# One adaLN unit less ahead of the first main step, the fold matrix first on VectorE, and matmuls on ones in three places

## The chip, the cores and the metric

The kernel runs on one core of a Trainium2 chip. Five engines of the core work side by side, each through its own queue in program order: TensorE (PE in the profile, with its weight loads listed apart as PEld), VectorE (DVE), ScalarE (ACT), GpSimd (POOL) and SyncE (SP), which issues the transfers from the chip's main memory. An engine waits only where its next instruction waits for a semaphore. The metric is the device time of one execution in microseconds (us), lower is better. Three runs of the kernel before took 1697.41, 1698.73 and 1699.22 us, so the median is 1698.73 us.

## The reference

Two layers of a diffusion backbone over 256 latent tokens and 256 context tokens of width 1024, all in float32. Layer 0 mixes tokens with a Conformer convolution, layer 1 with a bidirectional mLSTM; each is followed by a squared-ReLU MLP. What matters here is how a layer begins: a vector of shifts, scales and gates (adaLN) is computed from a conditioning vector by one large matrix, and the tokens are modulated with it before the first product.

```python
def adaln(cvec, w, b):
    return jnp.split(jax.nn.silu(cvec) @ w + b, 6, axis=-1)

def modulate(x, shift, scale):
    return x * (1 + scale) + shift

def conformer_conv(u, rows, w_pw1, b_pw1, w_dw, b_dw, ln_g, ln_b, w_pw2, b_pw2):
    a = u @ w_pw1 + b_pw1
    a = a[..., :CONV_DIM] * jax.nn.sigmoid(a[..., CONV_DIM:])
    ...
    a = jax.nn.silu(layer_norm(a + b_dw, ln_g, ln_b))
    return a @ w_pw2 + b_pw2

for i in range(DEPTH):
    ...
    sh1, sc1, g1, sh2, sc2, g2 = adaln(c[:, None, :], ada_w[i], ada_b[i])
    u = modulate(h, sh1, sc1)
```

## The kernel before

Activations lie transposed in SBUF: eight tiles of 128 channels by 512 tokens (latent and context side by side). A product in float32 accuracy is made of three matmuls on operands split into a high and a low part (`mm3`): high weight by high data, high weight by low data, low weight by high data. `split` makes such a pair: ScalarE copies the source to the high part (`wh` for weights), VectorE subtracts to get the low part (`wl`).

**The opening** works through eight units f, one for each 128 input channels. For a unit, SyncE issues three transfers: `raw`, the 128x2048 piece of the adaLN matrix for this unit's shift and scale; `x`, its 128x512 tokens; and `F`, a 128x512 piece of the first weight matrix `pw1`. Then

- `start0` runs eight float32 matmuls of 32 columns (`ada_mm`, the rows `fl<-raw,cs`), and VectorE copies the sum to SBUF (`F<-fl`);
- `start1` folds the four row groups of that sum with two small matmuls against the matrix `fold` (`ada_fold`, the rows `ln<-fold,F`); VectorE adds the biases (`sh1p`, `sc1p`); ScalarE makes the high part of the modulated tokens (`u`, two halves) while VectorE makes a full copy (`S`) and from it the low part (`u<-S,u`); the weight piece is split too;
- `start2` is the main step: four output tiles m (`ps0`, three PSUM tiles tagged `mm` and one tagged `cv`), three matmuls of 128x512 each, twelve in all.

The loop in the kernel before issues fold f-1, unit f's adaLN matmuls, and main step f-2, in this order, and `pin` fixes PE's order to that of the code. So three units' adaLN matmuls and two folds stand ahead of the first main step. The other engines' orders come from a scheduler; VectorE's also takes in the work of lower priority that follows (`foldg`, `pc`, and the sine tables `tab`). The tile pools set when transfers may start: `raw` has three buffers and `F` five.

After the opening the remaining twelve output tiles of `pw1` follow, 24 matmuls each, with transposes and small products between them.

**The place of the later waits** is the end of the convolution. VectorE ends a token normalisation (`mv`), it and ScalarE apply it (`apply_norm`), PE turns the result by transposes (`silu`, the rows `ln<-ident,u`), ScalarE applies SiLU and splits, and the products with `pw2` start in the PSUM tile `lead2[0]`. Just ahead of the transposes PE runs the last adaLN matmuls of this layer (`ada_s2.mm`, eight of them on tiles `S` and `L`).

## Time and profile before

| | us |
|---|---|
| median of three runs | 1698.73 |
| the profiled execution, whole | 1699.18 |
| its span, first to last instruction | 1697.5 |
| PE busy in the span | 1669.2 |
| DVE busy | 1033.0 |
| ACT busy | 744.0 |

The 1.7 us between the span and the whole time of the profiled execution lie before its first and after its last instruction. A row of the timeline gives the start in us from the span's start, the duration (of a row with "xN", that of N instructions merged), the engine, the line, the operation, what is written and read, and in brackets how long the engine had been idle and what ended it. A float32 matmul is shown as two instructions, so `x16` for the eight adaLN matmuls of a unit. The durations of matmuls overlap, since they are pipelined; what one costs in a row of equals is the distance of their starts. A row of the windows view gives, for a stretch of time, its length, each engine's busy time with the number of instructions, the granted PE clock (1.00 is full), the busy share of the transfer engines, and the GB/s they moved.

### The profile page before, as it was taken

Reading aid. Unit: us, or ns where it says so; the run is one execution under the profiler, and the core shown is the slowest. Engines: PE = TensorE matmul, PEld = TensorE weight load, DVE = VectorE, ACT = ScalarE, POOL = GpSimd, SP = SyncE. Lnnn points to the kernel's source line nnn. Section 1 sums busy time; section 2 is a strip of 40 time slices with the busy share of each in tenths; the row PEclk is TensorE's granted clock in tenths of the full one; section 3 lists DMA queues with packets and bytes.
Section 4 is the critical chain, followed back from the end, with each engine's and each line's share of the span. In section 5 each row is a group of like instructions: output and inputs, shape, how many; then the busy total and the mean of one; then the engine's idle time right before and its main releaser. Section 6 shows DMA issues by size and latency. Waiting matters only on the chain.

```text
span 1697.5 us, 22796 instructions
## 1 busy us (share of the span) xinstructions
PE 1669.2 (98%) x8878; PEld 1363.8 (80%) x8878; DVE 1033.0 (61%) x1841; ACT 744.0 (44%) x1195; POOL 44.3 (3%) x92
## 2 busy tenths in 40 slices
PE   7999999999999999999999999999999999999997
PEld 5655898878888998876788899888877878878886
DVE  5555795666645776751243653563487786776676
ACT  3312563232324476642333533442477564645443
POOL 0000000000000000000000000000011120000001
PEclk9999999999999999999999999999999999999999
DMA  8546322434424065567765752454454556756552
GB/s 340 198 156 243 111 75 95 157 128 146 145 100 148 2 211 180 183 238 252 251 214 174 251 181 105 155 189 171 157 190 176 193 195 209 257 211 229 192 184 89
DMA packets 70828, 300.54 MB, mean 177 GB/s; under 512 B 7170, under 2 KB 22018, under 8 KB 40384
## 3 DMA queue, kind: packets, MB, share of 16 engines
q1 hardware_dynamic: 53056, 284.39, 47.6%
q10 hardware_dynamic: 17664, 14.69, 2.7%
q8 instruction: 70, 1.15, 0.3%
q14 instruction: 38, 0.31, 0.1%
HBM read 283.32 MB, written 15.73 MB: 176 GB/s over the span
## 4 chain that ended last, share of the span: by engine, by line
PE 92%; DVE 5%; ACT 1%; issue 1%; DMA 1%; POOL 0%; SPq 0%; DVEq 0%; POOLq 0%; ACTq 0%
PE mm L175 17%; PE mm L178 17%; PE mm L179 17%; PE mm L190 7%; PE mm L191 4%; PE mm L206 3%; PE mm L207 3%; PE mm L208 3%; PE cv L208 2%; PE cv L207 2%; PE cv L206 2%; PE fl L335 1%; DVE wl L153 1%; PE fl L748 1%; PE cv L830 1%
## 5 line engine op out<-in xcount | busy, mean ns | idle before, releaser
L153 DVE TENSOR_TENSOR wl<-raw,wh 128x1024 fp32r<-128x1024 f32 x346 | 424.7, 1233 | 275.8 <-ACT wh L152 271.4
L152 ACT CAST wh<-raw 128x1024 fp32r<-128x1024 f32 x346 | 360.6, 1050 | 494.5 <-PE mm L178 269.0
L178 PE MATMUL mm<-u,wh 128*128 128x512 f32 (+1 forms) x808 | 292.9, 363 | 0.1
L175 PE MATMUL mm<-u,wh 128*128 128x512 f32 (+1 forms) x680 | 245.5, 361 | 0.2 <-ACT E L770 0.2
L179 PE MATMUL mm<-u,wl 128*128 128x512 f32 (+1 forms) x680 | 242.3, 357 | 0.0
L178 PEld LDWEIGHTS mm<-u,wh 128*128 128x128 f32 x808 | 153.4, 190 | 23.5 <-issue 1.8
L175 PEld LDWEIGHTS mm<-u,wh 128*128 128x128 f32 x680 | 129.2, 190 | 28.8 <-issue 9.1
L179 PEld LDWEIGHTS mm<-u,wl 128*128 128x128 f32 x680 | 129.2, 190 | 18.4 <-issue 0.2
L175 PE MATMUL mm<-xm,wh 128*128 128x512 f32 x256 | 102.2, 399 | 0.0
L206 PE MATMUL mm<-wh,xl 128*128 128x512 f32 x256 | 101.3, 396 | 0.5 <-ACT wh L152 0.5
L207 PE MATMUL mm<-wh,xl 128*128 128x512 f32 x256 | 100.9, 394 | 0.0
L179 PE MATMUL mm<-xm,wl 128*128 128x512 f32 x256 | 99.9, 390 | 0.0
L208 PE MATMUL mm<-wl,xl 128*128 128x512 f32 x256 | 99.6, 392 | 0.0
L175 PE MATMUL mm<-hid,wh 128*128 128x512 f32 (+1 forms) x256 | 93.1, 364 | 0.0
L178 PE MATMUL mm<-hid,wh 128*128 128x512 f32 (+1 forms) x256 | 92.8, 363 | 0.0
L179 PE MATMUL mm<-hid,wl 128*128 128x512 f32 (+1 forms) x256 | 92.7, 362 | 0.0
L190 PE MATMUL mm<-x,wh 128*128 128x512 f32 x232 | 81.0, 398 | 0.8 <-DVE x L1698 0.8
L416 DVE SCALAR_TENSOR_TENSOR S<-ar,cs,S 128x512 f32<-128x512 f32 x56 | 40.8, 749 | 61.3 <-DMA ar<-ada_w 61.0
L178 PE MATMUL mm<-qq,wh 128*128 128x272 f32 x256 | 73.9, 289 | 0.0
L175 PE MATMUL mm<-qq,wh 128*128 128x272 f32 x256 | 73.5, 289 | 0.0
L179 PE MATMUL mm<-qq,wl 128*128 128x272 f32 x256 | 73.5, 288 | 0.0
L190 PE MATMUL mm<-u,wh 128*128 128x512 f32 x192 | 68.6, 399 | 0.0
(507 smaller groups left out, 3277.8 us busy)
## 6 DMA issues: line engine op xcount, KB each, us to landing
raw<-w SPq DMA_DIRECT2D x64, 1024.0 KB, 4.8
raw<-wo SPq DMA_DIRECT2D x32, 1024.0 KB, 4.9
raw<-ada_w SPq DMA_DIRECT2D x26, 1024.0 KB, 5.9
ar<-ada_w SPq DMA_DIRECT2D x80, 256.0 KB, 3.4
raw<-wv SPq DMA_DIRECT2D x16, 1024.0 KB, 5.4
raw<-wqT SPq DMA_DIRECT2D x16, 1024.0 KB, 5.6
raw<-wq SPq DMA_DIRECT2D x16, 1024.0 KB, 4.9
raw<-wk SPq DMA_DIRECT2D x16, 1024.0 KB, 5.2
```

What stands on the lines that cost most here:

```text
L152: c = nc.scalar.copy(hi, src)
L153: nc.vector.tensor_tensor(lo, src, hi.bitcast(F32), op=ALU.subtract)
L175: a = nc.tensor.matmul(ps, wh, xh, start=start, stop=False)
L178: nc.tensor.matmul(ps, wh, xl, start=False, stop=False)
L179: lastmm[0] = nc.tensor.matmul(ps, wl, xh, start=False, stop=stop).ins
L190: todo = [lambda s_, e_: nc.tensor.matmul(ps, wh, r[0], start=s_, stop=e_), lambda s_, e_: nc.tensor.matmul(ps[:, :n], wl, r[0][:, :n], st ...
L191: lambda s_, e_: nc.tensor.matmul(ps[:, :n], wl, r[0][:, :n], start=s_, stop=e_)]
L206: nc.tensor.matmul(ps, xh, wh, start=start, stop=False)
L207: nc.tensor.matmul(ps, xl, wh, start=False, stop=False)
L208: nc.tensor.matmul(ps, xh, wl, start=False, stop=stop)
L335: a = nc.tensor.matmul(ps[32 * j:32 * j + 32], cs[:, kt, 14 - 2 * v:46 - 2 * v], blocks[kt], start=first and kt < 4, stop=last and kt >= 4 ...
L416: nc.vector.scalar_tensor_tensor(a, w, c, a, op0=ALU.mult, op1=ALU.add)
```

## The change

Six edits, all in the order of work; no product of the reference is added or taken away.

1. The opening's loop issues adaLN 0, fold 0, adaLN 1 and then, for each f, the first three matmuls of main step f, fold f+1, the other nine, and adaLN f+2. Two units' adaLN matmuls and one fold stand ahead of the first main step.
2. `idle(ps, n)` issues n matmuls of the 128x128 tile `ones` by itself into a PSUM tile that nobody reads before it is overwritten: 13 ahead of adaLN 0, 3 ahead of fold 0, 5 ahead of adaLN 1.
3. `foldg`, which is used much later, moves to the work of low priority, and the copy of the adaLN sum may not be issued on VectorE before `fold` is complete.
4. The weight piece is split after that copy and before the biases, which now wait in the order for the split's subtraction.
5. The fold's matmuls are fixed in PE's order.
6. At the end of the convolution `lead2` is allocated earlier, and five matmuls on ones go behind the last adaLN matmul, three more behind the turn of block 3.

```diff
@@ -136,12 +136,7 @@
     fold = con.tile([P, 16], F32, name="fold")
     nc.vector.tensor_tensor(fold, ident[:, 0:16], ident[:, 32:48], op=ALU.add)
     for j in (2, 3):
-        nc.vector.tensor_tensor(fold, fold, ident[:, 32 * j:32 * j + 16], op=ALU.add)
-    foldg = con.tile([P, 16], F32, name="foldg")
-    nc.vector.tensor_tensor(foldg, ident[:, 0:16], ident[:, 16:32], op=ALU.add)
-    for j in range(2, 8):
-        nc.vector.tensor_tensor(foldg, foldg, ident[:, 16 * j:16 * j + 16], op=ALU.add)
-
+        folded = nc.vector.tensor_tensor(fold, fold, ident[:, 32 * j:32 * j + 16], op=ALU.add).ins
 
     def raw_load(src):
         raw = wp.tile([P, 2048], F32, tag="raw", name=nm("raw"), bufs=3)
@@ -150,9 +145,10 @@
 
     def split(hi, lo, src):
         c = nc.scalar.copy(hi, src)
-        nc.vector.tensor_tensor(lo, src, hi.bitcast(F32), op=ALU.subtract)
+        lastsub[0] = nc.vector.tensor_tensor(lo, src, hi.bitcast(F32), op=ALU.subtract).ins
         return c.ins
 
+    lastsub = [None]
     anchors = []
 
     def split_w(src, make=None):
@@ -170,6 +166,13 @@
         return hi, lo
 
     pin = [False]
+
+    def idle(ps, n):
+        for _ in range(n):
+            a = nc.tensor.matmul(ps[:, 0:P], ones, ones, start=True, stop=True)
+            if pin[0]:
+                tc.keep_in_program_order(a)
+        return a.ins
 
     def mm3(ps, wh, wl, xh, xl, start, stop):
         a = nc.tensor.matmul(ps, wh, xh, start=start, stop=False)
@@ -329,10 +332,12 @@
         nc.vector.tensor_tensor(cs[:, :, 14 + i], sgc[:, i * DT:(i + 1) * DT], cc[:, i * DT:(i + 1) * DT], op=ALU.mult)
     ada = [con.tile([P, 48, 2], F32, name=f"ada{l}") for l in range(2)]
 
+    mark_unit = [None]
+
     def ada_mm(ps, blocks, v=0, first=True, last=True, kts=range(DT)):
         for kt in kts:
             j = kt % 4
-            a = nc.tensor.matmul(ps[32 * j:32 * j + 32], cs[:, kt, 14 - 2 * v:46 - 2 * v], blocks[kt],
+            a = mark_unit[0] = nc.tensor.matmul(ps[32 * j:32 * j + 32], cs[:, kt, 14 - 2 * v:46 - 2 * v], blocks[kt],
                                  start=first and kt < 4, stop=last and kt >= 4, tile_position=(0, 32 * j))
             if pin[0]:
                 tc.keep_in_program_order(a)
@@ -340,8 +345,10 @@
     def ada_fold(sb, n, nu=1, tag="fl"):
         tr = psum(tag)
         for b in range(n // P):
-            nc.tensor.matmul(tr[:, 2 * nu * b:2 * nu * (b + 1)], sb[:, b * P:(b + 1) * P], fold[:, 0:2 * nu],
-                             start=True, stop=True)
+            a = nc.tensor.matmul(tr[:, 2 * nu * b:2 * nu * (b + 1)], sb[:, b * P:(b + 1) * P], fold[:, 0:2 * nu],
+                                 start=True, stop=True)
+            if pin[0]:
+                tc.keep_in_program_order(a)
         return tr
 
     def ada_load(l, u, make=None, halves=(0, 1)):
@@ -623,30 +630,40 @@
         ps = psum("fl")[:, :2 * P]
         ada_mm(ps, [raw[:, kt * 2 * P:(kt + 1) * 2 * P] for kt in range(DT)])
         sb = F()[:, :2 * P]
-        nc.vector.tensor_copy(sb, ps)
-        st[f] = wr, sb
+        with tc.issue_after(folded):
+            st[f] = wr, sb, nc.vector.tensor_copy(sb, ps).ins
 
     def start1(f):
+        with tc.issue_after(st[f][2]):
+            w = split_w(st[f][0][:, 0:KO0 * P])
         tr = ada_fold(st[f][1], 2 * P, tag="ln")
-        nc.vector.tensor_scalar(sh1[:, :, f], tr[:, 0:2], vecs[:, o0 + f:o0 + f + 1], None, op0=ALU.add)
-        nc.vector.tensor_scalar(sc1[:, :, f], tr[:, 2:4], vecs[:, o0 + DT + f:o0 + DT + f + 1], 1.0,
-                                op0=ALU.add, op1=ALU.add)
+        with tc.issue_after(lastsub[0]):
+            nc.vector.tensor_scalar(sh1[:, :, f], tr[:, 0:2], vecs[:, o0 + f:o0 + f + 1], None, op0=ALU.add)
+            nc.vector.tensor_scalar(sc1[:, :, f], tr[:, 2:4], vecs[:, o0 + DT + f:o0 + DT + f + 1], 1.0,
+                                    op0=ALU.add, op1=ALU.add)
         u.append((U(F32R), U(F32R)))
         affine_split(*u[f], x[f], sc1, sh1, f)
-        st[f] = split_w(st[f][0][:, 0:KO0 * P])
-
-    def start2(f):
-        for m in range(KO0):
+        st[f] = w
+
+    def start2(f, ms):
+        for m in ms:
             mm3(ps0[m], *kcol(st[f], m), *u[f], f == 0, f == DT - 1)
 
     pin[0] = Z.pin0
-    for f in range(DT + 2):
-        if 0 <= f - 1 < DT:
-            start1(f - 1)
-        if f < DT:
-            start0(f)
-        if f >= 2:
-            start2(f - 2)
+    spare = psum("cv")
+    idle(spare, 13)
+    start0(0)
+    idle(spare, 3)
+    start1(0)
+    idle(spare, 5)
+    start0(1)
+    for f in range(DT):
+        start2(f, (0,))
+        if f + 1 < DT:
+            start1(f + 1)
+        start2(f, (1, 2, 3))
+        if f + 2 < DT:
+            start0(f + 2)
     pin[0] = False
 
 
@@ -654,6 +671,10 @@
 
     later = tc.high_priority(-100)
     later.__enter__()
+    foldg = con.tile([P, 16], F32, name="foldg")
+    nc.vector.tensor_tensor(foldg, ident[:, 0:16], ident[:, 16:32], op=ALU.add)
+    for j in range(2, 8):
+        nc.vector.tensor_tensor(foldg, foldg, ident[:, 16 * j:16 * j + 16], op=ALU.add)
     HL = L // 2
     ij = F()
     fj, jj = ij[:, 0:L], ij[:, L:2 * L]
@@ -932,6 +953,9 @@
         ada_s2.mm(last, range(4, 8))
         ada_s2.mm(more)
         ada_s2.mm(half + rest, range(4))
+    lead2 = [psum(), psum("cv")]
+    with tc.issue_after(mark_unit[0].ins):
+        idle(lead2[0], 5)
     sact = {0: [], 1: []}
 
     def silu(s):
@@ -956,7 +980,8 @@
 
     for _ in silu(0):
         pass
-    lead2 = [psum(), psum("cv")]
+    with tc.issue_after(mark["turn", 3]):
+        idle(lead2[0], 3)
     ob = psum("cv")
     with tc.issue_after(mark["norm", 0, 0]):
         products(1, 2)```

The change moves instructions at three places that the prediction speaks of; the rows that follow are of the program's order, `L` and the line of each program's own text. The first is PE's start. Before (`raw` and `cs` make the adaLN sums `fl`; `fold` and the copied sum `F` make `ln`; `u`, `wh` and `wl` are the operands of the main step):

```order
L335 MATMUL fl_125<-raw_120,cs 32x256 x8
L343 MATMUL ln_136<-fold,F_134 128x2 x2
L335 MATMUL fl_159<-raw_154,cs 32x256 x8
L343 MATMUL ln_170<-fold,F_168 128x2 x2
L335 MATMUL fl_193<-raw_188,cs 32x256 x8
L175 MATMUL mm_113<-u_141,wh_149 128x512
L178 MATMUL mm_113<-u_142,wh_149 128x512
L179 MATMUL mm_113<-u_141,wl_150 128x512
```

And in the change:

```order
L172 MATMUL cv_111<-ones 128x128 x13
L340 MATMUL fl_131<-raw_126,cs 32x256 x8
L172 MATMUL cv_111<-ones 128x128 x3
L348 MATMUL ln_149<-fold,F_140 128x2 x2
L172 MATMUL cv_111<-ones 128x128 x5
L340 MATMUL fl_173<-raw_168,cs 32x256 x8
L178 MATMUL mm_105<-u_154,wh_145 128x512
L181 MATMUL mm_105<-u_155,wh_145 128x512
L182 MATMUL mm_105<-u_154,wl_146 128x512
L348 MATMUL ln_191<-fold,F_182 128x2 x2
L178 MATMUL mm_106<-u_154,wh_145 128x512
```

The third adaLN group has moved behind the first main step, the second fold into it, and the ones stand ahead of what used to come after a wait.

The second place is VectorE up to the first biases. Before:

```order
L329 TENSOR_TENSOR cs<-sgc,vecs 128x8 x2
L153 TENSOR_TENSOR wl_150<-F_123,wh_149 128x512
L137 TENSOR_TENSOR fold<-ident 128x16
L141 TENSOR_TENSOR foldg<-ident 128x16
L626 COPY F_134<-fl_125 128x256
L139 TENSOR_TENSOR fold<-fold,ident 128x16
L143 TENSOR_TENSOR foldg<-foldg,ident 128x16
L667 TENSOR_SCALAR pc<-pc 128x1
L139 TENSOR_TENSOR fold<-fold,ident 128x16
```

And in the change:

```order
L332 TENSOR_TENSOR cs<-sgc,vecs 128x8 x2
L137 TENSOR_TENSOR fold<-ident 128x16
L675 TENSOR_TENSOR foldg<-ident 128x16
L139 TENSOR_TENSOR fold<-fold,ident 128x16
L677 TENSOR_TENSOR foldg<-foldg,ident 128x16
L139 TENSOR_TENSOR fold<-fold,ident 128x16
L634 COPY F_140<-fl_131 128x256
L148 TENSOR_TENSOR wl_146<-F_129,wh_145 128x512
L641 TENSOR_SCALAR sh1p<-ln_149,vecs 128x2
L642 TENSOR_SCALAR sc1p<-ln_149,vecs 128x2
```

`fold` and the copy stand ahead of the weight's low part `wl`, which waited for a transfer and had both behind it.

The third place is PE at the end of the convolution, from the last two adaLN matmuls on. Before (`ln<-ident,u` are the transposes, `mm_1358` is the first tile of `lead2`):

```order
L335 MATMUL fl_960<-S_1272,cs 32x512
L335 MATMUL fl_960<-L_1274,cs 32x512
L944 MATMUL ln_1296<-ident,u_566 128x128 x2
L944 MATMUL ln_1313<-ident,u_566 128x128
L944 MATMUL ln_1296<-ident,u_564 128x128 x2
L944 MATMUL ln_1313<-ident,u_566 128x128
L944 MATMUL ln_1313<-ident,u_564 128x128 x2
L944 MATMUL ln_1328<-ident,u_567 128x128 x2
L175 MATMUL mm_1358<-u_1303,wh_1177 128x256
```

And in the change:

```order
L340 MATMUL fl_982<-S_1294,cs 32x512
L340 MATMUL fl_982<-L_1296,cs 32x512
L172 MATMUL mm_1316<-ones 128x128 x5
L968 MATMUL ln_1325<-ident,u_588 128x128 x2
L968 MATMUL ln_1325<-ident,u_586 128x128 x2
L968 MATMUL ln_1342<-ident,u_588 128x128 x2
L968 MATMUL ln_1342<-ident,u_586 128x128 x2
L172 MATMUL mm_1316<-ones 128x128 x3
L968 MATMUL ln_1357<-ident,u_589 128x128 x2
L178 MATMUL mm_1316<-u_1332,wh_1199 128x256
```

The five ones stand between the last adaLN matmul and the transposes of the first two blocks of tokens, the three ones between these and the next transposes; the eight transposes are grouped by the tile they write. On every engine the order is the same as before from here to the program's end. Between the opening and this place, VectorE's order is shifted in some twenty rows around the sine tables: the copy of unit 7 is followed by three table rows, the weight split and the biases, and the product row `E` of the second output tile after the opening stands behind the last table row and ahead of the next weight split, where before it stood behind that split.

## The prediction

> **What bounds the kernel now.** I read the page first: its head and the chain of work that ended last.
>
> ```profile
> span 1697.5 us, 22796 instructions
> ...
> PE 92%; DVE 5%; ACT 1%; issue 1%; DMA 1%; POOL 0%; SPq 0%; DVEq 0%; POOLq 0%; ACTq 0%
> ```
>
> TensorE carries 92% of the chain, so time is won where it waits, or where it works slowly. The timeline of the first 17 us shows both.
>
> ```profile
> 0.90 0.17 DVE L128 MEMSET ones<- 128x128 f32 x1 [0.90 <-PEq L1877]
> ...
> 6.67 1.94 PE L335 MATMUL fl<-raw,cs 128*32 128x256 f32 x16 [6.67 <-DMA raw<-ada_w]
> ...
> 8.00 0.62 ACT L152 CAST wh<-F 128x512 fp32r<-128x512 f32 x1 [2.28 <-DMA F<-pw1a]
> ...
> 8.64 0.69 DVE L153 TENSOR_TENSOR wl<-F,wh 128x512 fp32r<-128x512 f32 x1 [4.25 <-ACT wh L152]
> ...
> 9.42 0.42 DVE L626 COPY F<-fl 128x256 f32<-128x256 f32 x1
> ...
> 10.21 1.02 PE L343 MATMUL ln<-fold,F 128*128 128x2 f32 x4 [1.60 <-DVE fold L139]
> ...
> 11.15 1.94 PE L335 MATMUL fl<-raw,cs 128*32 128x256 f32 x16
> ...
> 11.26 0.22 DVE L631 TENSOR_SCALAR sh1p<-ln,vecs 128x2 f32<-128x2 f32 x1 [0.81 <-PE ln L343]
> ...
> 11.73 1.09 ACT L597 ACTIVATE u<-x,sh1p,sc1p 128x256 fp32r<-128x256 f32 x2 [3.12 <-DVE sc1p L632]
> ...
> 12.86 0.69 DVE L600 TENSOR_TENSOR u<-S,u 128x512 fp32r<-128x512 f32 x1
> ...
> 16.75 0.79 PE L175 MATMUL mm<-u,wh 128*128 128x512 f32 x1
> ```
>
> PE stands still until the first `raw` lands at 6.67. Then fold 0 waits 1.60 us, because VectorE first stood before the weight's low part (8.64, which waits for a transfer), and the copy of the sum (9.42) and `fold` lay behind it. The first main step starts at 16.75, behind two folds and three units' adaLN matmuls. And all of this runs at half speed, which the windows show by counts, not by the clock column:
>
> ```profile
> 16.60:20.00 3.40, 3.40 (x12) 2.58 (x9) 1.62 (x3) 0.37 (x1) 0.00 (x0) 1.00 1.03 410
> 20.00:23.40 3.40, 3.40 (x30) 2.45 (x29) 1.30 (x5) 1.34 (x3) 0.00 (x0) 1.00 1.02 405
> ```
>
> 12 instructions in 3.4 us, then 30 in the next 3.4 us, both with a clock of 1.00: before its first change the column tells nothing. The same adaLN group shows it too: 1.94 us at 6.67 and 11.15, 1.00 us below (30.14 to 31.14). The steady steps:
>
> ```profile
> 22.57 0.50 PE L175 MATMUL mm<-u,wh 128*128 128x512 f32 x1
> ...
> 26.86 0.50 PE L175 MATMUL mm<-u,wh 128*128 128x512 f32 x1
> 27.19 0.39 PE L178 MATMUL mm<-u,wh 128*128 128x512 f32 x1
> ...
> 29.48 0.39 PE L179 MATMUL cv<-u,wl 128*128 128x512 f32 x1
> ...
> 29.71 0.50 PE L343 MATMUL ln<-fold,F 128*128 128x2 f32 x4
> ...
> 30.14 1.07 PE L335 MATMUL fl<-raw,cs 128*32 128x256 f32 x16
> ...
> 31.14 0.50 PE L175 MATMUL mm<-u,wh 128*128 128x512 f32 x1
> ...
> 39.72 0.50 PE L175 MATMUL mm<-u,wh 128*128 128x512 f32 x1
> ...
> 42.93 0.49 PE L175 MATMUL mm<-u,wh 128*128 128x512 f32 x1
> ...
> 46.04 0.19 PEld L178 LDWEIGHTS mm<-u,wh 128*128 128x128 f32 x1 [0.28 <-DVE u L600]
> ...
> 48.45 0.39 PE L179 MATMUL cv<-u,wl 128*128 128x512 f32 x1
> ```
>
> A step with a fold and an adaLN group takes 31.14 - 26.86 = 4.28 us, one with a fold alone 42.93 - 39.72 = 3.21, so an adaLN group costs 1.07. Within a step matmuls are 0.23 apart, the first 0.33. Twelve take 29.48 - 26.86 + 0.23 = 2.85, so a fold costs 0.36. The last slot of the opening ends at 48.45 + 0.23 = 48.68.
>
> The other place is the end of the convolution, by windows and timeline:
>
> ```profile
> 166.80:170.20 3.40, 1.93 (x12) 1.43 (x13) 2.54 (x5) 2.74 (x6) 0.00 (x0) 1.00 1.01 426
> 170.20:173.60 3.40, 3.40 (x17) 3.23 (x16) 1.19 (x3) 3.12 (x9) 0.00 (x0) 0.51 0.70 296
> ```
> ```profile
> 167.41 1.06 PE L944 MATMUL ln<-ident,u 128*128 128x128 f32 x8 [1.25 <-DVE u L860]
> ...
> 169.26 0.44 PE L944 MATMUL ln<-ident,u 128*128 128x128 f32 x2 [0.78 <-ACT S L947]
> ...
> 170.41 1.16 ACT L947 ACTIVATE S<-ln,vecs 128x256 f32<-128x256 f32 x2
> ...
> 173.74 1.94 PE L830 MATMUL cv<-E,tab 128*64 128x512 f32 x8
> ```
>
> PE waits 1.25 and 0.78 us, and then runs 3.4 us at 0.51 of its clock. Ten of the twelve instructions in the window ahead of the fall are transposes.
>
> **The opening, part by part.** A matmul on ones is two passes with a 128x128 load. Four such loads take 11.15 - 10.21 = 0.94 us cold (0.24 each) and 30.14 - 29.71 = 0.43 warm (0.11); 128 columns of streaming are half of a 256-column pass of the adaLN group, which is four passes deep: 1.94 / 8 = 0.24 cold, 1.00 / 8 = 0.13 warm. So one costs 0.48 us cold and 0.25 warm. Ones are ready at 0.90 + 0.17 = 1.07; thirteen end between 4.4 (all warm) and 7.3 (all cold). The transfer lands at 6.67: this edit costs 0 to 0.6 us, hidden by the load. In return the clock should be open by then: cold main matmuls opened it in the stretch from 16.75 to about 20, 3.3 us of dense work, and here are 5.6. What opens it is not shown for matmuls on ones; I come back to that.
>
> The chain then runs: adaLN 0 ends at 7.7 to 8.3 (1.00 warm), the copy takes 0.42 with nothing of VectorE's ahead of it, three ones 0.75, the fold 0.43: 8.9 to 9.6. The biases stand behind the weight's low part, whose transfer does not move: 8.64 + 0.69 = 9.33. From the first bias to `u` is 11.73 - 11.26 = 0.47 us, from there to the end of its low part 12.86 + 0.69 - 11.73 = 1.82, the small VectorE rows between being about as many. So the operands of step 0 are there at 9.33 + 0.47 + 1.82 = 11.6. PE fills with five ones (1.25, to 10.2 to 10.9) and adaLN 1, whose data had landed by 11.15 at the latest, since that row shows no wait: it ends between 11.2 and 12.2. I take 11.9 for step 0 (range 11.4 to 12.6).
>
> What follows from there, against before:
> - step 0 starts 16.75 - 11.9 = 4.85 us earlier;
> - it runs warm: 22.57 - 16.75 - 4.28 = 1.54 us less;
> - one adaLN group and one fold now come after it: 1.07 + 0.36 = 1.43 more;
> - each of the seven folds now interrupts a step, with one more slow first matmul: 7 x 0.10 = 0.7 more;
> - step 7 waits for its low part, as it did before for 0.28 (the row at 46.04):
>
> ```profile
> 40.94 0.42 DVE L626 COPY F<-fl 128x256 f32<-128x256 f32 x1
> ...
> 45.30 0.68 DVE L600 TENSOR_TENSOR u<-S,u 128x512 fp32r<-128x512 f32 x1
> ```
>
> From that copy to the end of the low part were 45.30 + 0.68 - 40.94 = 5.04 us on VectorE, with the sine tables between. In the new order three table rows of about 1.0 us together go behind it, which leaves 4.0. The copy starts some 0.1 after adaLN 7, so the part is there 4.1 after it; PE asks for it after a step with fold, the added restart and a first matmul, 3.21 + 0.10 + 0.33 = 3.6. That is 0.5 of waiting, 0.2 more than before.
>
> Sum of the opening: 4.85 + 1.54 - 1.43 - 0.7 - 0.2 = 4.06 us gained; I take 3.9, since the operands of steps 1 to 6 are now made during one step instead of more. Their slack: copy 0.42 (plus 0.1), ScalarE's half of the split 0.62, VectorE's 0.69, then 0.47 + 1.82, in all 4.1 us from the end of a unit's adaLN, against 4.28 + 0.10 + 0.33 = 4.7 until PE needs them. So 0.6 us to spare, and no wait.
>
> Transfers: a unit is 1.57 MB (`raw` 128x2048, `x` and `F` 128x512 each, four bytes), 3.85 us at the 405 to 410 GB/s of the two windows above, less than the new period of 4.38. Unit 1 is there by 11.15, so unit 2 by 15.0; PE asks for it at 11.9 + 3.3 = 15.2, and every later one with 0.5 more to spare. SyncE's queue keeps its order, and what its transfers wait for (adaLN and fold three units back) comes earlier throughout. A rate lower by a tenth would cost 0.2 to 2 us here.
>
> Behind the opening the gain has to pass VectorE, which is almost full, and a place where PE waited for it:
>
> ```profile
> 50.00:60.00 10.00, 10.00 (x50) 8.32 (x49) 9.79 (x22) 3.39 (x6) 1.99 (x8) 1.00 0.88 311
> ...
> 100.00:120.00 20.00, 19.78 (x97) 11.96 (x96) 13.14 (x31) 3.37 (x4) 0.00 (x0) 1.00 0.34 123
> ...
> 140.00:160.00 20.00, 20.00 (x90) 11.09 (x90) 8.37 (x12) 4.75 (x6) 0.00 (x0) 1.00 0.56 206
> ```
> ```profile
> 62.90 0.63 PE L777 MATMUL ln<-ident,E 128*128 128x128 f32 x4 [0.36 <-DVE E L774]
> ```
>
> This `E` stood behind a weight split that waited for a transfer; in the new order it stands ahead of that split, right behind the tables. So I expect the 0.36 us of waiting not to grow; 0 taken, between 0.3 gained and 1.0 lost. From there to the convolution's end PE has hardly a wait (19.78 of 20 us and 20.00 of 20 in the two later windows), so the rest moves along.
>
> **The later waits.** Five ones warm are 1.25 us in a wait of 1.25, three are 0.75 in one of 0.78: 0 to 0.3 lost by overrun. If the clock then stays open, the way to the `cv` row at 173.74 is set by ScalarE: the last transposes need a PSUM tile that the activation at 170.41 frees at 171.57, four of them take 0.4 to 0.5, so `cv` starts near 172.1. Gain 1.6, less 0.2 for overrun: 1.4 taken, between 1.7 (all of 3.4 x 0.49) and -0.3. Does it stay open? This window held it:
>
> ```profile
> 1504.70:1508.10 3.40, 2.32 (x15) 1.94 (x16) 3.16 (x12) 2.42 (x8) 0.00 (x0) 1.00 0.93 363
> ```
> ```profile
> 1505.01 1.09 PE L1683 MATMUL ln<-ident,res 128*128 128x128 f32 x8 [1.32 <-DVE res L1651]
> ```
>
> There PE was busy for 2.32 us, of which 1.09 with transposes, so 1.2 us of other matmuls were enough. In the window that lost the clock the 1.93 us less 1.06 and 0.44 of transposes leave 0.4. The ones add some 1.3 (0.55 of the five still fall into it, and the three), which makes 1.7.
>
> A rule that speaks against this edit: the Trainium skill, page "TensorE: Matmul & The Clock Gate", section "Why this matters for your kernels", lets the clock drop only for gaps of PE of more than about 3 us. By that the gaps of 1.25 and 0.78 here could not close it, and filling them would gain nothing; the trace has it closed all the same. The same page's part on PE transposes says that they do not count as busy, by which the gap would run from 166.16 past 169.26, over 3.1 us, and the trace would agree.
>
> **Sum.** The profiled execution took 1699.18 us (span 1697.5), 0.45 above the median. 1699.18 - 3.9 - 1.4 = 1693.9; from the median 1693.4. I say 1693.8.
>
> **Rivals.**
> - *The later ones buy nothing* (chance 0.14): the clock falls anyway, or the row of ScalarE was the limit all along, and the overrun costs 0.2. For it: the busy time of the window that lost the clock was 1.93 us, so busy time alone does not hold it. Against it: the window at 1504.70. Time 1699.18 - 3.9 + 0.2 = 1695.5.
> - *The steps wait for their operands* (0.14): one unit less ahead leaves 0.6 us of slack, and with VectorE's `pc` and `foldg` rows in the first units, or a transfer late, the chain is 1.0 us longer. Steps 0 to 5 then lose 0.4 each, 2.4 in all. Against it: VectorE has no other work in the steady steps until the tables. Time 1693.9 + 2.4 = 1696.3.
> - *Ones do not open the clock* (0.10), and the change is slower. Thirteen end at 7.3, adaLN 0 at 9.2, copy and three cold ones at 10.7, a cold fold at 11.6, the operands at 14.0, five cold ones at 14.0, adaLN 1 at 15.9. Step 0 then starts only 0.85 earlier and as cold as before, and the 1.43, 0.7 and 0.2 remain: 1.5 lost. The later ones lose 0.3. Time 1699.2 + 1.8 = 1701.0. It decides from the point where the clock is still half at adaLN 1. For it: a fold and an adaLN group from 10.21 to 13.09, 2.9 us of PE on end, did not open it. Against it: those groups use 32 columns of the array and the folds stream two columns, while ones fill it.
>
> **How the numbers follow.** The forecast has 0.62, and its own range is 1692.0 to 1695.4. The range of 1691.9 to 1697.0 takes in the first two rivals and leaves out the third and the tails, under 2 in 10. A measurement here tells a change of about 0.2%, 3.4 us, from none, which puts the bound at 1695.3. Faster: 0.60 of the forecast, 0.07 and 0.04 of the first two, 0.71 in all. Slower by as much (above 1702.1) is half of the third, 0.05 with tails 0.06. The rest, 0.23, is no change.
>
> **What would show it.** In the new trace: thirteen matmuls on ones from about 1.1 whose spacing halves before 8; adaLN 0 and 1 at 1.0 us each; fold 0 ahead of 9.7; step 0 at 11.4 to 12.6 with matmuls 0.23 apart; periods of 4.4; the opening's end near 44.8; the transposes of the row at 62.90 near 59; a clock of 1.00 from 165 to 175 and the first `cv` row there 5.3 us earlier than 173.74. The forecast is wrong if step 0 starts after 14, if waits on VectorE or on transfers stand in steps 1 to 6, or if the clock still falls after the ones.

## The result, and the profile after

The changed kernel took 1694.03 us (median of 13 runs, 1693.57 to 1695.45), the kernel before 1698.49 us in the 13 runs beside it (1697.30 to 1699.22): ratio 0.9976, 95% interval 0.9969 to 0.9983. A second set on another chip gave 1693.87 against 1698.11 us, 0.9973 (0.9962 to 0.9983). The profiled execution took 1694.03 us against 1699.18, and its span is 5.2 us shorter.

The page's head and its chain of work that ended last:

```profile
span 1692.3 us, 22908 instructions
...
PE 91%; DVE 5%; ACT 1%; DMA 1%; issue 1%; POOL 0%; SPq 0%; DVEq 0%; POOLq 0%; ACTq 0%
```

TensorE still sets the end. The timeline of the opening (start, duration, engine and line, tiles, and in brackets the idle time ahead and what ended it):

```profile
1.12 5.46 PE L172 MATMUL cv<-ones 128*128 128x128 f32 x26 [1.12 <-DVE ones L128]
...
6.61 1.07 PE L340 MATMUL fl<-raw,cs 128*32 128x256 f32 x16
...
7.74 0.42 DVE L634 COPY F<-fl 128x256 f32<-128x256 f32 x1 [2.85 <-PE fl L340]
...
8.38 0.51 PE L348 MATMUL ln<-fold,F 128*128 128x2 f32 x4
8.49 0.69 DVE L148 TENSOR_TENSOR wl<-F,wh 128x512 fp32r<-128x512 f32 x1 [0.33 <-ACT wh L147]
...
10.48 1.07 PE L340 MATMUL fl<-raw,cs 128*32 128x256 f32 x16 [0.37 <-DMA raw<-ada_w]
10.65 0.69 DVE L607 TENSOR_TENSOR u<-S,u 128x512 fp32r<-128x512 f32 x1
11.48 0.50 PE L178 MATMUL mm<-u,wh 128*128 128x512 f32 x1
...
15.91 0.50 PE L178 MATMUL mm<-u,wh 128*128 128x512 f32 x1
```

The thirteen ones stand in the list as 26 passes. The adaLN groups take 1.07 us, not 1.94: the clock is open. The copy follows its sum at once and the fold waits for nothing. Step 0 starts at 11.48 us instead of 16.75, and step 1 4.43 us later. The last step, and the two places behind the opening:

```profile
41.58 0.51 PE L178 MATMUL mm<-u,wh 128*128 128x512 f32 x1
42.31 0.51 PE L181 MATMUL mm<-u,wh 128*128 128x512 f32 x1 [0.22 <-DVE u L607]
...
44.72 0.39 PE L182 MATMUL cv<-u,wl 128*128 128x512 f32 x1
...
46.31 0.63 PE L798 MATMUL ln<-ident,E 128*128 128x128 f32 x4 [0.30 <-DVE E L795]
...
58.60 0.66 PE L798 MATMUL ln<-ident,E 128*128 128x128 f32 x4
```

The opening ends at 44.72 + 0.23 = 44.95 against 48.68. The transposes that stood at 62.90 with a wait of 0.36 stand at 58.60 without one. The end of the convolution:

```profile
161.61 0.59 PE L340 MATMUL fl<-L,cs 128*32 128x512 f32 x1
162.14 1.38 PE L172 MATMUL mm<-ones 128*128 128x128 f32 x10
163.45 1.06 PE L968 MATMUL ln<-ident,u 128*128 128x128 f32 x8
164.35 0.83 PE L172 MATMUL mm<-ones 128*128 128x128 f32 x6
165.19 0.44 PE L968 MATMUL ln<-ident,u 128*128 128x128 f32 x2
...
168.18 1.94 PE L851 MATMUL cv<-E,tab 128*64 128x512 f32 x8
```
```profile
162.96:166.37 3.41, 3.33 (x25) 2.75 (x25) 2.42 (x5) 2.87 (x7) 0.00 (x0) 1.00 1.01 428
166.37:169.79 3.42, 3.42 (x24) 2.11 (x22) 1.29 (x4) 3.15 (x9) 0.00 (x0) 1.00 0.73 302
```

In the windows the columns after the length are the busy times of PE, its weight loads, VectorE, ScalarE and GpSimd, each with its count, then the granted clock, the share of the DMA engines and GB/s. The clock stays at 1.00. The `cv` row starts 5.56 us earlier than at 173.74, and 6.57 us behind the last adaLN row (161.61) where it was 8.18 behind (165.56).

Matched by their PE rows, the two profiled executions stand apart by 3.95 us from 140 on and by 5.54 from 180 to 1220. About 0.35 is given back between 1220 and 1245, where VectorE holds TensorE up twice by 0.2 us (the rows at 1223.70 and 1234.42), and 5.2 remain at the end.

### The profile page after: what moved, and what is told of

Its sections match the earlier page's. It is cut to its first block, busy times and chain, and to the rows that moved or that the text cites. A ratio compares the mean times of both kernels' runs of the same rounds, so it can differ in the third digit from the quotient of the medians.

```text
span 1692.3 us, 22908 instructions
## 1 busy us (share of the span) xinstructions
PE 1673.3 (99%) x8936; PEld 1368.1 (81%) x8936; DVE 1034.3 (61%) x1841; ACT 744.8 (44%) x1195; POOL 44.3 (3%) x92
## 4 chain that ended last, share of the span: by engine, by line
PE 91%; DVE 5%; ACT 1%; DMA 1%; issue 1%; POOL 0%; SPq 0%; DVEq 0%; POOLq 0%; ACTq 0%
PE mm L178 17%; PE mm L181 17%; PE mm L182 17%; PE mm L193 7%; PE mm L194 4%; PE mm L211 3%; PE mm L210 3%; PE mm L209 3%; PE cv L211 2%; PE cv L209 2%; PE cv L210 2%; PE fl L340 1%; DVE wl L148 1%; PE fl L769 1%; PE cv L851 1%
## 5 line engine op out<-in xcount | busy, mean ns | idle before, releaser
L148 DVE TENSOR_TENSOR wl<-raw,wh 128x1024 fp32r<-128x1024 f32 x346 | 425.0, 1233 | 278.0 <-ACT wh L147 275.7
L147 ACT CAST wh<-raw 128x1024 fp32r<-128x1024 f32 x346 | 360.7, 1050 | 502.1 <-PE mm L181 271.1
L181 PE MATMUL mm<-u,wh 128*128 128x512 f32 (+1 forms) x808 | 292.0, 362 | 0.3 <-DVE u L607 0.2
L178 PE MATMUL mm<-u,wh 128*128 128x512 f32 (+1 forms) x680 | 244.8, 361 | 0.0
L182 PE MATMUL mm<-u,wl 128*128 128x512 f32 (+1 forms) x680 | 241.5, 356 | 0.0
L181 PEld LDWEIGHTS mm<-u,wh 128*128 128x128 f32 x808 | 152.6, 189 | 23.7 <-issue 1.8
L178 PEld LDWEIGHTS mm<-u,wh 128*128 128x128 f32 x680 | 128.5, 189 | 27.4 <-issue 9.2
L182 PEld LDWEIGHTS mm<-u,wl 128*128 128x128 f32 x680 | 128.4, 189 | 18.8 <-issue 1.0
L178 PE MATMUL mm<-xm,wh 128*128 128x512 f32 x256 | 102.2, 399 | 0.0
L182 PE MATMUL mm<-xm,wl 128*128 128x512 f32 x256 | 99.9, 390 | 0.0
L178 PE MATMUL mm<-hid,wh 128*128 128x512 f32 (+1 forms) x256 | 93.1, 364 | 0.0
L181 PE MATMUL mm<-hid,wh 128*128 128x512 f32 (+1 forms) x256 | 92.8, 363 | 0.0
L182 PE MATMUL mm<-hid,wl 128*128 128x512 f32 (+1 forms) x256 | 92.8, 362 | 0.0
L181 PE MATMUL mm<-qq,wh 128*128 128x272 f32 x256 | 73.9, 289 | 0.0
L178 PE MATMUL mm<-qq,wh 128*128 128x272 f32 x256 | 73.5, 289 | 0.0
L182 PE MATMUL mm<-qq,wl 128*128 128x272 f32 x256 | 73.5, 288 | 0.0
```

Of the source, the lines that this page charges most:

```text
L147: c = nc.scalar.copy(hi, src)
L148: lastsub[0] = nc.vector.tensor_tensor(lo, src, hi.bitcast(F32), op=ALU.subtract).ins
L178: a = nc.tensor.matmul(ps, wh, xh, start=start, stop=False)
L181: nc.tensor.matmul(ps, wh, xl, start=False, stop=False)
L182: lastmm[0] = nc.tensor.matmul(ps, wl, xh, start=False, stop=stop).ins
```

## The experiments

All landmarks in one table, each from one profiled execution: the start of step 0, the end of the opening (its last slot and 0.23), how far the first `cv` row of the convolution's end starts behind the last adaLN row, where a stretch of half clock lies (that of the idle end left out), and the time of the profiled run beside the median of all runs of that kernel (where it was run more than once). The tests e9 and e10 have a paragraph of their own.

| kernel | step 0 | end | cv behind | half clock | profiled | median |
|---|---|---|---|---|---|---|
| before | 16.75 | 48.68 | 8.18 | 170.24 | 1699.18 | 1698.49 |
| changed | 11.48 | 44.95 | 6.57 | none | 1694.03 | 1694.03 |
| e1, no later ones | 11.21 | 44.73 | 6.67 | 1245.56 | 1695.76 | 1695.84 |
| e13, the same | 11.69 | 45.15 | 8.17 | 166.38, 1504.40 | 1698.15 | |
| e14, the same | 11.47 | 44.97 | 6.67 | 1502.2 | 1696.18 | |
| e2, only later ones | 16.39 | 47.36 | 6.56 | none | 1695.70 | 1697.23 |
| e3, no ones in the opening | 12.15 | 48.41 | 6.57 | 1506.47 | 1699.83 | 1698.14 |
| e4, of those only the 13 | 11.28 | 44.56 | 6.57 | none | 1693.97 | 1696.19 |
| e8, a unit more ahead | 14.95 | 46.93 | 6.58 | 15.14 | 1696.42 | 1696.36 |
| e12, fold and copy first alone | 15.91 | 46.97 | 7.74 | 167.50 | 1697.10 | 1697.84 |
| e11, changed and five more near 1500 | 11.11 | 44.61 | 6.57 | none | 1693.23 | 1694.05 |
| e15, changed, again | 11.24 | 44.70 | 6.58 | 1245.63 | 1695.48 | 1693.87 |

Medians compare only on one chip: the kernel before had 1699.23 us beside e1, e2, e3 and e8 (35 runs, from 1696.12 to 1702.38), 1698.24 beside e4 and e11, 1698.66 beside e12, and 1698.11 beside e15. Since these runs spread by more than the effects, what follows is read from landmarks first. Each landmark is one execution of its kernel.

**The later ones (e1, e2, e13, e14).** e1 takes the eight ones out of the changed kernel, e2 puts them alone into the kernel before; e13 and e14 run e1's kernel again.

```diff
-    lead2 = [psum(), psum("cv")]
-    with tc.issue_after(mark_unit[0].ins):
-        idle(lead2[0], 5)
...
-    with tc.issue_after(mark["turn", 3]):
-        idle(lead2[0], 3)
+    lead2 = [psum(), psum("cv")]
```

> The changed kernel without the eight ones in the two later waits; the opening is the changed one. Theory (the ones keep the clock open there): the opening ends at 44.95 as in the changed kernel, the clock falls to about half in one window of 3.4 us near 166 to 170, and the first cv row comes 1.26 us later than the changed kernel's 168.18, near 169.4: 1695.3 us. Rival (the later ones buy nothing: the opening's 4.3 us of lead already moves the two waits to another place against the clock's windows, so that each window holds some 1.6 us of other matmuls): the clock stays 1.00 from 160 to 172, cv near 168.2, 1694.0 us.

> The kernel before with the eight ones in the two later waits alone; its opening is the old one (step 0 at 16.75 us, end at 48.68). Theory: the clock stays 1.00 from 165 to 176, the cv row comes 1.3 to 1.4 us earlier than 173.74, near 172.4, and the time is 1698.5 - 1.3 = 1697.2 us. Rival (the ones buy nothing): cv at 173.7 to 173.9 and 1698.5 to 1698.7 us.

> The kernel without the later ones once more, another execution. Theory (the clock's windows of 3.41 us lie elsewhere against the program in each execution; without the later ones it falls where a window holds the most of the two waits): step 0 and the opening as in the changed kernel, and near 165 to 173 either a fall, with the first cv row 1.4 to 1.7 us later than it is 6.6 us behind the end of the last adaLN group, or none, as in the first execution, where it was 6.67 behind. Rival (the changed opening has moved the waits for good): never a fall.

> The kernel without the later ones a third time; the same two theories: a fall near 165 to 173 with the cv row 1.4 to 1.7 us late, or none, by the place of the windows, against never a fall.

e2 did as its theory said: 1697.23 us, `cv` 6.56 behind instead of 8.18 (ratio to before 0.9992, 0.9983 to 1.0000, so by the times alone it would be open). Its `cv` row came at 170.26, earlier than the 172.4 expected, since its opening happened to end at 47.36 instead of 48.68; more on this below. e1 went the rival's way at this place: no fall, `cv` 6.67 behind. Its time of 1695.76 has other causes, a half clock from 1245.56 on and a transfer of `wo` that held TensorE up for 0.86 near 1442. e14 was like e1, and e13 showed the fall:

```profile
163.66 1.06 PE L965 MATMUL ln<-ident,u 128*128 128x128 f32 x8 [1.25 <-DVE u L881]
165.50 0.44 PE L965 MATMUL ln<-ident,u 128*128 128x128 f32 x2 [0.78 <-ACT S L968]
...
169.98 1.94 PE L851 MATMUL cv<-E,tab 128*64 128x512 f32 x8
```
```profile
162.96:166.38 3.42, 1.86 (x12) 1.37 (x13) 2.63 (x5) 2.77 (x6) 0.00 (x0) 1.00 1.01 424
166.38:169.79 3.41, 3.41 (x17) 3.39 (x17) 1.19 (x3) 3.13 (x9) 0.00 (x0) 0.50 0.77 322
```

The changed kernel's execution shown further up has its windows at the same place (162.96 to 166.37), and its program ran only 0.2 us ahead of e13's: with the ones PE is busy for 3.33 us there and keeps the clock, without them for 1.86 and loses it. That is the cause of this part, side by side. But the same kernel loses the clock here in one execution and keeps it in two. Of five profiles without later ones (before, e1, e12, e13, e14) three have the fall; of the seven with all eight (changed, e2, e3, e4, e8, e11, e15) none. A fall costs 8.17 - 6.67 = 1.50 us, in e12 only 7.74 - 6.67 = 1.07. Where there is none, the ones bring 0.10.

**The ones of the opening (e3, e4).** e3 takes out all 21, e4 the 3 and the 5.

```diff
-    spare = psum("cv")
-    idle(spare, 13)
     start0(0)
-    idle(spare, 3)
     start1(0)
-    idle(spare, 5)
     start0(1)
```

> The changed kernel without the 13, 3 and 5 ones of the opening; order of units, copy and fold as changed, later ones kept. Theory (the order gives the early start, the ones the clock): adaLN 0 at 6.67 takes 1.94 us, the fold 0.94, adaLN 1 1.94 again, step 0 starts near 12.6 instead of 11.48 and runs at half speed for some 3.4 us, 1.5 us lost: the opening ends 2.6 later than 44.95, near 47.5, and the time is 1694.0 + 2.6 = 1696.6 us. Rival (the ones of the opening bring nothing, the order all): step 0 at 11.5 to 12, warm by its spacing of 0.23, end near 45.2, 1694.0 to 1694.3 us.

> The changed kernel without the 3 and the 5 ones between adaLN 0, fold 0 and adaLN 1; the 13 in the loading time and the later ones kept. Theory (the clock is set anew every 3.41 us by how busy TensorE was in the window before, and these windows lie elsewhere against the program in each execution): the window from about 7 to 11 us then holds adaLN 0's rest, a fold and adaLN 1, some 2 us of narrow matmuls in 3.41, little more than the 1.79 that closed the clock in the run with one unit more ahead; the clock falls before or in step 0, up to 3.4 us at half, the opening ends up to 1.7 us later than 44.95, and the time is 1694.0 + 1.6 = 1695.6 us. Rival (thirteen are enough): no fall, the opening's end within 0.3 of 44.95, 1694.0 us.

e3 follows the theory, and more so. The order alone brings step 0 to 12.15, but cold, and the clock opens only at 18.3:

```profile
12.15 0.80 PE L178 MATMUL mm<-u,wh 128*128 128x512 f32 x1
...
17.87 0.58 PE L182 MATMUL cv<-u,wl 128*128 128x512 f32 x1
18.37 1.07 PE L340 MATMUL fl<-raw,cs 128*32 128x256 f32 x16
```

The opening ends 48.41 - 44.95 = 3.46 us later (2.6 expected), only 0.27 ahead of the kernel before in its profile, and its median of 1698.14 us lies 1.5 above the 1696.6 expected. Without the ones the new order brings next to nothing. In e4's profile the rival held: no fall, and the end 0.39 earlier, where adaLN 1 had its transfer 0.2 earlier (10.28). The runs say otherwise: median 1696.19 (1693.97, the profiled one, to 1699.68), while e11 below, on the same chip, had 1694.05. That the 3 and the 5 hold the clock in other executions fits this, but no profile shows it.

**The unit, and the fold first (e8, e12).** e8 puts the unit back ahead of step 0 and keeps the rest; e12 is e8 without any ones.

```diff
     start0(1)
+    start1(1)
+    start0(2)
     for f in range(DT):
-        start2(f, (0,))
-        if f + 1 < DT:
-            start1(f + 1)
-        start2(f, (1, 2, 3))
-        if f + 2 < DT:
-            start0(f + 2)
+        start2(f, range(KO0))
+        if f + 2 < DT:
+            start1(f + 2)
+        if f + 3 < DT:
+            start0(f + 3)
```

> The changed kernel with the one adaLN unit ahead of the first main step put back (adaLN 2 and fold 1 before step 0, folds between the steps again and not inside them); ones, copy and fold of the opening and the later ones kept. Theory (the early start is worth the whole: TensorE would wait for unit 2's transfer until about 15): step 0 near 16.2 at full speed, 4.7 later, less the adaLN group, fold and restart that are now ahead of it (1.5) and seven restarts (0.7): the opening ends 2.4 later, near 47.4, 1696.4 us. Rival (where the unit stands is worth nothing, the ones and the fold first are all): opening's end within 0.5 of 44.95, 1694.0 to 1694.5 us. Third: TensorE's wait for the transfer closes the clock again and step 0 is cold, 1.5 more: 1697.9 us.

> Of the whole change only the fold matrix and the copy first on VectorE (with foldg behind): the units in the old order, one more ahead, no ones anywhere. Theory (unit 2's transfer, not the fold, sets step 0 in this order): fold 0 waits 0.5 us instead of 1.60, but adaLN 2 starts only when its data lands, near 14, runs cold for 1.9 us, and step 0 starts near 15.9 instead of 16.75, cold until the clock opens: 0.8 us gained at most, 1697.7 us; no ones in the later waits, so the clock near 166 to 174 falls or not by where its windows lie. Rival (the 1.60 us wait of the fold is gained whole): step 0 near 15.1, 1696.9 us.

In e8 TensorE waits for unit 2's transfer and the mechanism of the third case sets in, by timeline and windows:

```profile
13.95 1.07 PE L340 MATMUL fl<-raw,cs 128*32 128x256 f32 x16 [1.62 <-DMA raw<-ada_w]
14.95 0.64 PE L178 MATMUL mm<-u,wh 128*128 128x512 f32 x1
...
20.83 0.50 PE L178 MATMUL mm<-u,wh 128*128 128x512 f32 x1
```
```profile
11.73:15.14 3.41, 1.78 (x21) 1.20 (x22) 2.81 (x12) 1.31 (x3) 0.00 (x0) 1.00 1.03 406
15.14:18.56 3.42, 3.42 (x9) 2.67 (x9) 1.06 (x2) 0.62 (x1) 0.00 (x0) 0.50 1.04 411
```

Its opening ends 1.98 later than the changed kernel's. Of that 20.83 - 14.95 - 4.28 = 1.60 is the half clock and 0.4 the order itself. So in this execution leaving the unit out pays mainly because TensorE then does not idle for a transfer with the clock just opened. The median of 1696.36 us is that of the first theory (1696.4) and not of the third (1697.9), but by chance: the transfer landed at 13.95 and not near 15, which gave back what the clock took. e12 put step 0 where its theory had it (15.91, 15.9 expected), and its median of 1697.84 is no change that can be told (ratio 0.9997, 0.9987 to 1.0006).

The ends of the opening in the table make a square of four, all with the fold matrix first. In the old order it ends at 46.97 without ones (e12) and at 46.93 with them (e8); in the new order at 48.41 without (e3) and at 44.95 with them (changed). So neither the ones nor the new order gains by itself here, and together they gain 2.0 us over e12: the ones open the clock, and the new order leaves no wait behind them in which it closes again.

**Do transposes hold the clock? (e9, e10)** The five ones of the first later wait become 40 transposes, or 40 ones.

```diff
+    def idle_t(ps, n):
+        for _ in range(n):
+            nc.tensor.transpose(ps[:, 0:P], ones, ident)
...
-        idle(lead2[0], 5)
+        idle_t(lead2[0], 40)
```

> The changed kernel with the five ones of the first later wait replaced by 40 transposes of 128x128, long enough to hold a whole window of 3.41 us wherever the windows lie. It asks whether transposes keep the clock. Theory (they do not count): the 40 start warm, 0.27 us each, and run at 0.53 from the end of the first whole window on; the clock column falls to 0.50 within 7 us, the 40 take some 14 to 16 us instead of 10.6, and the run takes 1694.0 + 14 = 1708 us or more. Rival (they count as any other matmul): clock 1.00, 10.6 us, first cv row 9.3 later than 168.2, 1703.3 us.

> The control to the 40 transposes: 40 matmuls on ones in the same place. Both theories: clock 1.00 from 160 to 185, the 40 take 40 x 0.27 = 10.6 us, first cv row 9.3 us later than the changed kernel's 168.2, 1694.0 + 9.3 = 1703.3 us. If the clock falls here too, ones do not hold it either and the theory of the later waits falls.

The control behaved, if cheaper: 40 ones in 9.20 us, 0.23 each, clock 1.00, 1701.28 us. The transposes took one pass each, 0.115 us and not the 0.27 expected, the run took 1696.93 us instead of the rival's 1703.3, and the clock stayed:

```profile
162.04 4.58 PE L179 MATMUL mm<-ident,ones 128*128 128x128 f32 x40
```
```profile
161.71:165.12 3.41, 3.41 (x32) 3.09 (x29) 2.98 (x9) 0.82 (x1) 0.00 (x0) 1.00 0.99 408
165.12:168.53 3.41, 3.40 (x31) 3.12 (x29) 0.09 (x1) 1.43 (x4) 0.00 (x0) 1.00 1.02 430
```

The first is one whole window of the clock in this execution (by the end's fall at 1690.9, 448 windows of 3.413 later), and 3.08 of its 3.41 us are transposes. It kept the clock, with 0.33 us of other matmuls in the window, where the kernel before lost it with 1.97 - 1.06 - 0.44 = 0.47. The theory that transposes do not count falls. That they count as much as other matmuls is not shown by this: the 40 stand without a gap, turn the constant tile `ones`, and fill the window nearly whole.

**The spread of the changed kernel (e11, e15).** Its 13 runs lie in two groups, seven from 1693.57 to 1694.03 and six from 1694.90 to 1695.45. e11 adds five ones in waits near 1500 us; e15 is the changed kernel once more.

```diff
-    def turn(t, g_, tag="ln"):
+    def turn(t, g_, tag="ln", ones_first=0):
...
         tr = psum(tag)
+        if ones_first:
+            idle(tr, ones_first)
...
-        ln1(turn(1, 0), 1, 0)
+        ln1(turn(1, 0, ones_first=5), 1, 0)
```

> The changed kernel with five more ones near the end, in TensorE's waits of 0.51 and 1.32 us ahead of the transposes of the rows near 1500 us (one and four of them). Theory (executions of the changed kernel lie 1.4 us apart because the clock still falls in some of them near 1506 or 1245): no fall near 1506 in this profile, the step of 1.5 us that such a fall adds there is gone, the fastest runs stay as they are (1693.6 us on the first chip) and the median comes 0.3 to 0.7 us nearer to them: 1694.0 less 0 to 0.5. Rival (the ones overrun the waits, or the two groups of runs have another cause): no gain, 1694.0 to 1694.5 us, with as wide a spread.

> The changed kernel itself once more, for its second group of executions (1.4 us above the first on the first chip). Theory (a wo transfer that lands 1.2 to 1.4 us later near 1441, as in the runs without the later ones and in the run with thirteen ones alone): if this profile is of the slower group, TensorE waits 0.7 to 0.9 us for the cast of a wo block near 1441 and the clock stays 1.00 up to 1680. Rival (a fall of the clock near 1245 or 1506): then a window of 3.4 us at 0.50 stands there and no such wait. If the profile is of the faster group, neither, and it stays open. The middle in every case: the first cv row 6.57 us behind the end of the last adaLN group, clock 1.00 from 160 to 176.

e11's profile has no fall, but its nine runs stay in two groups (1693.23 to 1694.05, 1695.04 to 1695.66), with a median of 1694.05: no gain that can be told, the rival's result. e15's profile fell into the slower group, and not by a late transfer, as the theory had it, but by the rival's half clock:

```profile
1242.22:1245.63 3.41, 2.76 (x12) 1.34 (x11) 2.83 (x6) 3.37 (x5) 0.00 (x0) 1.00 0.11 41
1245.63:1249.04 3.41, 3.41 (x10) 2.67 (x9) 1.60 (x5) 3.36 (x7) 0.73 (x1) 0.50 0.92 312
```

It ends 1.43 us behind the first profile of the changed kernel; it was 0.30 ahead of it at 1242, 1.34 behind at 1250, and 1.13 behind at 1255. No version was found that beats the changed kernel.

## Why the prediction held, point by point

**The sum.** 3.9 us were taken for the opening and 1.4 for the later waits. In the profiles it is 3.95 (at 140 to 160 us) and 5.56 - 3.95 = 1.61, less the 0.35 given back near 1235. The medians differ by 4.46, less than the profiles. The half-clock stretches fit this: the changed kernel has one at 1245 in some of its executions, and that the kernel before has its fall at 170 in only some of its own is likely by e1, e13 and e14, but it was profiled once. That the sum came so near is in part luck: the earlier start brought 0.42 more than said and the later waits 0.2 more, the rest of the opening cost 0.75 more, and 0.35 went near 1235 for a reason that the prediction did not have.

**The price of the ones.** 0.48 cold and 0.25 warm were worked out. All thirteen ran cold in e14, from 1.12 to adaLN 0 at 6.96, 0.45 each; warm they are 0.23 (e10). The clock opened on ones in every profile that has them, before the end of adaLN 0 (its rows take 1.07 us, in e14 1.14), so the third rival (ones do not open it) was wrong, and e3 shows what it would have cost. That they are hidden by the load holds only in part: in the changed kernel, e1, e4, e10, e14 and e15 adaLN 0 shows no wait for its transfer, so the ones ended last, and the thirteen are about as many as fit.

**Step 0** came at 11.48, inside 11.4 to 12.6 and ahead of the 11.9 taken. The low part of the weight was through at 9.18 instead of 9.33, the operands at 11.34 instead of 11.6, and adaLN 1 started when its transfer landed (10.48, a wait of 0.37). So step 0 waits for adaLN 1, which ends 0.14 behind the operands, and its transfer, which had only a bound in the prediction (11.15 at the latest), sets it.

**The ledger.** Start earlier: 5.27 (4.85 said). Cold step: 1.54, as said, but this is one execution's draw; in e2, with the same opening as before, step 0 to step 1 took 21.24 - 16.39 = 4.85, 4.28 warm, so there it was only 0.57, and its opening ended at 47.36. Against that draw the changed opening gains 2.41 us, against the profile of before 3.73:

```profile
16.39 0.80 PE L182 MATMUL mm<-u,wh 128*128 128x512 f32 x1
...
21.24 0.50 PE L182 MATMUL mm<-u,wh 128*128 128x512 f32 x1
```

What comes after step 0 costs more than said: 5.27 + 1.54 - 3.73 = 3.08 against 1.43 + 0.7 + 0.2 = 2.33. This is the mis-sized term. A period is 4.43, not 4.38, so a fold inside a step costs 0.15 of restart and not 0.10, for seven of them 0.35 more. The rest lies in the last two steps (41.58 to 44.95 is 3.37 for step 7, whose twelve matmuls take 2.85), where 0.2 was said and 0.6 was lost. The wait of 0.28 in the row at 46.04, from which the 0.2 was taken, is that of a weight load (PEld), and the matmuls of before lost only some 0.1 there. No wait for operands or transfers stands in steps 1 to 6, so the second rival was wrong. The 0.36 at 62.90 went, as hoped, and a wait of 0.30 stands at 46.31 where 0.24 stood at 49.08.

**The later waits.** `cv` was expected 5.3 earlier and came 5.56 earlier. The number is in part luck, since the 1.4 was read from an execution that happened to have the fall. The mechanism was half right. Right: the ones keep the clock open, and the fall is what the 1.4 paid for (e2, e13). Wrong: the step by which the transposes in the window ahead of 170 do not count at all, so that only 0.4 us were left. e9 shows that they count; that they count for less fits the windows, as the last section shows. And the fall is no fixed property of the place: without the ones it came in three of five executions. So the first rival (they buy nothing) is true of single executions, 0.10 in e1 and e14, and wrong on the mean: 1.60 in two of five executions, 1.17 in e12 and 0.10 in two make 0.9 us, an estimate from five profiles.

The rule on gaps weighed in the prediction (the Trainium skill, "TensorE: Matmul & The Clock Gate", "Why this matters for your kernels": only idle gaps over some 3 us cost the clock) does not hold here: the fall of before came with no gap longer than 1.25 us, that of e15 with none over 0.65, and the longest gap ahead of any fall inside the program was 1.62 (e8). Nor does that page's part "PE-mode transpose" hold as it stands, by which the full clock does not engage for transposes, since they do not count as busy in the same way: 3.08 us of float32 transposes kept the clock in e9. What it says in "What's actually happening", that activity is judged in windows of 3413 ns which run freely against the program, agrees with every run: within one execution the falls lie whole windows apart (e13: 1504.40 - 166.38 = 1338.02, 392 times 3.413), and between executions they lie elsewhere.

## What to carry to other kernels

Work that does nothing can pay on the matrix engine where it stands in a wait, ahead of dense work, but here it paid only together with an order that kept the engine busy behind it (the ones alone 0.04 us, e8 against e12; the order alone 1.4 lost, e3 against e12; both 2.0 gained, each from one execution). A stretch of half clock seen in one profile is a draw: look at several executions before pricing it in full, and look for the same risk at every other place with waits close together. And when work is put ahead of a main loop to fill it, ask which transfer it waits for: one unit more (e8) idled the engine just long enough to lose the clock it had opened.

## What the runs showed of the hardware that had not been expected

The clock changed only at the bounds of a grid of 3.41 us, and every stretch of half clock between the first opening and the program's end lasted one step of it. The grid's place differs between executions of the same kernel, and a fall costs 1.1 to 1.6 us where it comes: that is the spread of the changed kernel as far as e15 shows it.

What a window must hold is not settled by busy time. Windows with 1.97 (before), 1.86 (e13) and 1.78 us (e8) of PE lost the clock, but so did one with 2.76, where transposes and matmuls with operands of 36 rows stand (e15, 1242.22), while two others kept it:

```profile
8.80:12.21 3.41, 1.93 (x21) 1.28 (x22) 3.07 (x20) 1.71 (x3) 0.00 (x0) 1.00 1.04 420
```
```profile
1241.57:1244.99 3.42, 2.78 (x13) 1.54 (x11) 3.34 (x7) 3.37 (x4) 0.00 (x0) 1.00 0.00 0
```

The first is e4's, and most of a gap of 1.77 us lies in it. The second is that of the changed kernel at the place where e15 lost it, with 0.02 us more; there the rows of 36 take 0.86 us, in e15 1.49. At the program's end the last matmuls, all 128x512, stand alone ahead of an idle engine, and show what such work needs. Two windows each, of the changed kernel and of e2:

```profile
1681.89:1685.31 3.42, 1.27 (x6) 0.73 (x4) 2.08 (x2) 0.00 (x0) 2.79 (x3) 1.00 0.21 77
1685.31:1688.72 3.41, 0.00 (x0) 0.00 (x0) 3.31 (x7) 0.29 (x1) 0.00 (x0) 0.50 0.21 77
```
```profile
1683.31:1686.72 3.41, 1.59 (x8) 0.97 (x6) 1.94 (x3) 0.00 (x0) 3.12 (x3) 1.00 0.21 77
1686.72:1690.13 3.41, 0.00 (x0) 0.00 (x0) 3.31 (x8) 0.30 (x1) 0.00 (x0) 1.00 0.22 79
```

1.27 us of them lose the clock for the next window, and 1.59 hold it, where 1.97 us with 1.50 of transposes (before) did not. So transposes seem to count for less than these, if it is the sum over a window that decides; their weight was not measured. What opens the clock is not settled either: e3's window from 11.43 to 14.84, busy throughout with cold work, was followed by another at half speed, while e12's from 13.91 to 17.32, busy for 3.28 us, opened it.

A float32 transpose of 128x128 takes half of what a float32 matmul of that shape takes, 0.115 against 0.23 us.

In four of the profiles (e1, e4, e13, e14) a transfer of `wo` near 1441 landed more than 1 us later than in the others, with the same order of instructions; why is open.
